# Encoder block with expert-choice experts: first token tiles split and normalized by VectorE alone, base tiles of the final normalization moved from GpSimd's to SyncE's DMA queue

## Chip, cores and metric

One core of a Trainium2 chip runs the whole program in one launch. The metric is the device time of that core in microseconds (us), the median of the runs shown. Five compute engines appear below: TensorE (PE; PEld is its weight load), VectorE (DVE), ScalarE (ACT), GpSimd (POOL) and SyncE (SP), which here issues DMAs only. Each engine works through its own instructions in program order and waits on semaphores of the others.

## What is computed

The input is 2048 tokens of 1024 channels in float32, with 16 learned meta tokens put in front. Cut to what matters here:

```
h    = layer_norm(concat([meta, x]), ln_in_g, ln_in_b)
proj = h @ w_in                       # q, k, v, u, two gates
...                                   # rms-normed q/k, rotary, attention; S5 scan; gated merge
h    = layer_norm(alpha * h + merged @ w_o, ln1_g, ln1_b)
# experts: each of 16 experts takes its 256 best tokens
gate, idx = top_k(softmax(h @ w_router, over tokens), 256)
xe  = h[idx]
ye  = (silu(xe @ w_gate[e]) * (xe @ w_up[e])) @ w_down[e] * gate
moe = zeros.at[idx].add(ye)
out = layer_norm(alpha * h + moe, ln2_g, ln2_b)
```

The changed code is at the two ends: the first layer norm with the first projection, and the last layer norm, which runs beside the last seven experts.

## The kernel before

**Arithmetic.** Float32 matmuls are made of rounded parts: an operand is cast to a high part on ACT (`wh`, `hth`, `xh`, `hh`) and DVE or POOL subtracts it from the original to get the low part (`wl`, `htl`, `xl`, `hl`). Three matmuls (high by high, low by high, high by low) give one product. The step that does this for a weight tile is called a split.

**Start (`phase_a`).** Tokens are worked in 16 tiles of 128 (and one of 16 meta tokens). `load(t)` fetches tile t, `norm(t)` normalizes it on DVE (`ln_ops`, eleven DVE instructions: two statistics, one aggregate, six small ones for the reciprocal root with one ACT square root among them, and two over the whole 128x1024 tile, L106 and L107). `trans(t)` transposes it on PE (L176) and splits the result (L183 ACT, L184 DVE). The projection weight comes in eight row blocks of 768 columns (half 0) and eight of 512 (half 1). `split_w(m, k, eng)` splits block k of half m: cast on ACT (L156), subtraction on `eng` (L157). Tiles 0 and 1 are normalized together, the first three blocks of half 0 are split on POOL and the other five on DVE; then `qkv` runs k by k. Half 1 is split by DVE and POOL in turn while PE works on the first two tiles. A loop over steps s then makes `trans(s+1)`, `norm(s+2)`, `rope(s-1)`, `qkv(s)` and `u_mm` for one tile after another; tile 3 is normalized in step s=1 of this loop.

**Experts.** For each expert e the 12 weight tiles (jobs) of 1 MB each are fetched by SP (`load_w`, L1684), cast on ACT (L1691) and subtracted on DVE (L1692). `ahead(j)` issues load j+3 and split j+2 when PE starts on job j. There are three buffers of the raw tile `wr`, so load j+3 waits on SP until the subtraction of job j is done. Eight steps with gate and up matmuls (L1784) are followed by eight with down matmuls (L1812), two of them for one weight tile. Tokens are gathered (`xg`, L1754) and results added into `acc_d` in DRAM (`scatter`, L1834) by indirect DMAs that POOL issues.

**Side work.** From expert 9 on, `step(e, s)` moves a list of generators on by one piece per PE step. `finish` normalizes the base tiles: all 16 tiles of `acc_d` are loaded (`fx`, L1900), normalized in pairs on ACT (L1874, L1880) and DVE (L1885, L1887) and stored to the output (L1915); a new pair starts every 11 steps, and the next pair's loads are issued in the middle of the pair before. `redo(e)` gathers again the rows that expert e added to (`fa`, L1846), normalizes them and writes them over the output rows (`put_rows`, L1890). For the last expert the same is done by tile in `down_out` (L1818 to L1827).

**What sets the order.** There is no planner: each engine's order is the order in which the code emits instructions, and a DMA is issued by the engine named in front of `dma_start`, in that engine's order. The lines of the change are these:

```
for k in range(3):
    split_w(0, k, PL)
...
if 2 < s + 2 <= NT:
    norm(s + 2)
...
PL.dma_start(xs[t], acc_d[128 * t:128 * t + 128])
...
PL.dma_start(outs[t + i], xs.pop(t + i))
```

Of the kernel before, what the change touches and what calls it, by code (L numbers as in the profile page):

```python
# [28 lines left out]
NT = S // 128  # L29
# [15 lines left out]
def f(t):  # L45
    return t.bitcast(F32)
# [3 lines left out]
def kernel(ctx, tc, x, meta, ln_in_g, ln_in_b, w_in, q_norm_g, k_norm_g,  # L50
# [5 lines left out]
    V, A, PE, PL, SP = nc.vector, nc.scalar, nc.tensor, nc.gpsimd, nc.sync  # L56
    ctx.enter_context(tc.manual_schedule())

    def pool(reuse_waits="tile", **kw):
        return tc.tile_pool(reuse_waits=reuse_waits, **kw)  # L60
# [13 lines left out]
    xs = x[0].rearrange("(c j) d -> j c d", j=T)  # L74
    outs = out[0].rearrange("(c j) d -> j c d", j=T)
# [22 lines left out]
    def ln_ops(pool, t, n, gb, bb, tag):  # L98
        st = pool.tile([128, 2, 6], F32, name=tag + "st", tag=tag + "st")
        mv = pool.tile([128, 2], F32, name=tag + "mv", tag=tag + "mv")  # L100
        r = pool.tile([128, 1], F32, name=tag + "r", tag=tag + "r")
        for i in range(2):
            yield V.bn_stats(st[:n, i], t[:n, 512 * i:512 * i + 512])
        yield V.bn_aggr(mv[:n], st[:n])
        yield from rsqrt_ops(pool, r, mv[:n, 1:2], eps_ln, LN_EPS, 1.0, n, tag)
        yield V.scalar_tensor_tensor(t[:n], t[:n], mv[:n, 0:1], gb[:n], op0=OP.subtract, op1=OP.mult)  # L106
        yield V.scalar_tensor_tensor(t[:n], t[:n], r[:n], bb[:n], op0=OP.mult, op1=OP.add)  # L107
# [5 lines left out]
    def layer_norm(*args):  # L113
        for _ in ln_ops(*args):
            pass

    def phase_a(start_gates):
        cr = ExitStack()
        with ExitStack() as c:
# [4 lines left out]
            sm = c.enter_context(pool(name="a_sm", bufs=3))  # L124
# [3 lines left out]
            X, HT, PQ, QN, RC = {}, {}, {}, {}, {}  # L128
# [10 lines left out]
            gb = wq.tile([128, D], F32, name="gb")  # L139
            bb = wq.tile([128, D], F32, name="bb")  # L140
# [13 lines left out]
            def split_w(m, k, eng):  # L154
                wr = WR.pop(0)
                A.copy(WH[m][:, k], wr)  # L156
                eng.tensor_tensor(WL[m][:, k], wr, f(WH[m][:, k]), op=OP.subtract)  # L157

            def norm(t):
                n = 128 if t < NT else NM  # L160
                layer_norm(sm, X[t], n, gb, bb, "a")
# [8 lines left out]
            def trans(t):  # L170
                n = 128 if t < NT else NM
                if 1 < t < NT:
                    SP.dma_start(h_d[128 * t:128 * t + 128], X[t])
                p = px.tile([128, 8, 128], F32, name="pT")
                for k in range(8):
                    PE.transpose(p[:, k, :n], X[t][:n, 128 * k:128 * k + 128], idf[:n, :n])  # L176
                if t == NT or t % 2 == 0:
                    HT[t // 2] = (hp.tile([128, 8, 256], F32R, name="hth", bufs=3),
                                  hp.tile([128, 8, 256], F32R, name="htl", bufs=3))
                hi, lo = HT[t // 2]  # L180
                o = 128 * (t % 2)
                for k0 in (0, 4):
                    A.copy(hi[:, k0:k0 + 4, o:o + n], p[:, k0:k0 + 4, :n])  # L183
                    V.tensor_tensor(lo[:, k0:k0 + 4, o:o + n], p[:, k0:k0 + 4, :n],  # L184
                                    f(hi[:, k0:k0 + 4, o:o + n]), op=OP.subtract)
                if 1 < t < NT and t % 2 == 1:
                    store_ht(t // 2)
# [5 lines left out]
            def qkv(t, k0, k1):  # L193
                n = 128 if t < NT else NM
                o = 128 * (t % 2)
                hi, lo = HT[t // 2]
                if k0 == 0:
                    PQ[t] = pq.tile([128, 1024], F32, name="pq")
                p = PQ[t]
                for k in range(k0, k1):  # L200
                    for c0, c1 in ((0, 512), (512, 768))[t == NT:]:
                        for i, (a, w) in enumerate(((hi, WH[0]), (lo, WH[0]), (hi, WL[0]))):
                            PE.matmul(p[:n, c0:c1], a[:, k, o:o + n], w[:, k, c0:c1],
                                      start=(k == 0 and i == 0), stop=(k == 7 and i == 2))
# [87 lines left out]
            with pool(name="a_st", bufs=8) as st:  # L292
                for k in range(8):
                    load_w(st, 0, k)
                load(2)
                for _ in zip(*(ln_ops(sm, X[t], 128, gb, bb, "a") for t in range(2))):
                    pass
                for k in range(3):
                    split_w(0, k, PL)
                trans(0)  # L300
                trans(1)
                qkv(0, 0, 2)
                qkv(1, 0, 2)
                for k in range(2, 8):
                    if k > 2:
                        split_w(0, k, V)
                    qkv(0, k, k + 1)
                    qkv(1, k, k + 1)
# [12 lines left out]
                load_w(wr, 1, k)  # L321
            load(3)
            norm(2)
            for k in range(8):
                split_w(1, k, (V, PL)[k % 2])
                if k + 3 < 8:
                    load_w(wr, 1, k + 3)
                if k == 4:
                    load_rope(2)
                    load_rope(3)  # L330
# [4 lines left out]
            for s in range(NT + 4):  # L335
                if s + 4 <= NT:
                    load(s + 4)
                    if s + 4 < NT:
                        load_rope(s + 4)
                if s < NT:  # L340
                    rope_prep(s)
                if 1 <= s < NT:
                    trans(s + 1)
                if 0 <= s - 3 < NT:
                    qk_trans(s - 3, 0)
                next(gg, None)
                if 1 < s <= NT:
                    qkv(s, 0, 3)
                next(gg, None)
                if 0 <= s - 3 <= NT:  # L350
                    qk_trans(s - 3, 1)
                next(gg, None)
                if 2 < s + 2 <= NT:
                    norm(s + 2)
                if 0 <= s - 1 <= NT:
                    rope(s - 1)
                if 1 < s <= NT:
                    qkv(s, 3, 8)
                if 1 <= s <= NT:
                    u_mm((s - 1) // 2, (s - 1) % 2)  # L360
                if s == NT:
                    cr.close()
                    gg = start_gates()
                    next(gg)
                    u_meta()
# [879 lines left out]
    acc_d = dram("acc_d", (S, D), F32)  # L1245
# [291 lines left out]
    E = 16  # L1537
# [133 lines left out]
    def experts(c, pos, inf):  # L1671
# [4 lines left out]
        W, X, XT, HT, IDX, IO, AC = {}, {}, {}, {}, {}, {}, {}  # L1676
# [10 lines left out]
        def split_w(j):  # L1687
            wr = W[j]
            wh = wp.tile([128, 8, 256], F32R, name="wh", bufs=4)
            wl = wp.tile([128, 8, 256], F32R, name="wl", bufs=4)  # L1690
            A.copy(wh, wr)  # L1691
            V.tensor_tensor(wl, wr, f(wh), op=OP.subtract)  # L1692
            W[j] = wh, wl
# [19 lines left out]
        sm = c.enter_context(pool(name="e_m", bufs=2))  # L1713
# [124 lines left out]
        gb = fp.tile([128, D], F32, name="gb2")  # L1838
        bb = fp.tile([128, D], F32, name="bb2")
# [53 lines left out]
        def finish():  # L1893
            SP.dma_start(gb, row_bcast(ln2_g, D))
            SP.dma_start(bb, row_bcast(ln2_b, D))
            xs = {}

            def load(t):
                xs[t] = fp.tile([128, D], F32, name="fx", bufs=4)
                PL.dma_start(xs[t], acc_d[128 * t:128 * t + 128])  # L1900

            yield
            for t in range(2):
                load(t)
            yield
            yield

            def base(t):
                for n, _ in enumerate(norm([xs[t], xs[t + 1]])):
                    if n == 7 and t + 2 < NT:  # L1910
                        load(t + 2)
                        load(t + 3)
                    yield
                for i in range(2):
                    PL.dma_start(outs[t + i], xs.pop(t + i))  # L1915

            yield from pipe((base(t) for t in range(0, NT, 2)), every=MO[3])

# [10 lines left out]
        sides = []  # L1929

        def step(e, s):
            if (e, s) == (E0, 0):
                sides.append(finish())
            if E0 < e < E - 1 and s == MO[0]:
                sides.append(redo(e - 1, MO[1]))
            if (e, s) == (E - 1, 1):
                acc_rows(e)
                sides.append(redo(e - 1, MO[2]))
            for g in sides:
                next(g, None)  # L1940

        one_hot(0, 0, NT)
        pi = pick(0)
# [187 lines left out]
```

## Time and profile before

| what | value |
|---|---|
| median of 3 runs | 3164.89 us (3157.53 to 3165.57) |
| profiled execution, its own time | 3158.51 us |
| its span in the trace | 3156.7 us |
| PE busy | 2978.7 us (94%) |
| DVE busy | 2145.9 us (68%) |
| ACT busy | 1572.0 us (50%) |
| POOL busy | 1010.9 us (32%) |
| DMA bytes | 513.00 MB, mean 163 GB/s |

The profiled execution is 6.4 us shorter than the median. Its own time is 1.8 us more than its span. DMA issue counts as no engine's busy time, so SP has no row. A wait is shown at the instruction behind it, as time its engine sat idle and what ended that.

### The profile page before, as it was taken

Reading aid. Unit: us, or ns where it says so; the run is one execution under the profiler, and the core shown is the slowest. Engines: PE = TensorE matmul, PEld = TensorE weight load, DVE = VectorE, ACT = ScalarE, POOL = GpSimd, SP = SyncE. Lnnn points to the kernel's source line nnn. Section 1 sums busy time; section 2 is a strip of 40 time slices with the busy share of each in tenths; the row PEclk is TensorE's granted clock in tenths of the full one; section 3 lists DMA queues with packets and bytes.
Section 4 is the critical chain, followed back from the end, with each engine's and each line's share of the span. In section 5 each row is a group of like instructions: output and inputs, shape, how many; then the busy total and the mean of one; then the engine's idle time right before and its main releaser. Section 6 shows DMA issues by size and latency. Waiting matters only on the chain.

```text
span 3156.7 us, 56179 instructions
## 1 busy us (share of the span) xinstructions
PE 2978.7 (94%) x22829; PEld 2632.0 (83%) x22829; DVE 2145.9 (68%) x3725; ACT 1572.0 (50%) x2229; POOL 1010.9 (32%) x633
## 2 busy tenths in 40 slices
PE   6999999999989999999899996799999999999997
PEld 5887787777867777777678885699999999999997
DVE  7886589783366666666466666666666665778886
ACT  2222352243369999999622222344444444666553
POOL 3221035051069999999510001111111101122221
PEclk9999999999999999999999998799999999999999
DMA  6566633557510101013366743366677667778884
GB/s 224 186 206 186 160 104 108 185 148 203 175 45 22 35 21 35 21 35 90 110 206 199 200 134 108 134 214 206 214 220 225 217 214 230 258 260 267 274 263 157
DMA packets 464499, 513.00 MB, mean 163 GB/s; under 512 B 47568, under 2 KB 387728, under 8 KB 463856
## 3 DMA queue, kind: packets, MB, share of 16 engines
q1 hardware_dynamic: 433616, 421.20, 42.7%
q0 software_dynamic: 19232, 69.53, 7.3%
q10 hardware_dynamic: 11392, 18.68, 1.7%
q8 instruction: 179, 2.93, 0.4%
q14 instruction: 80, 0.66, 0.1%
HBM read 385.59 MB, written 123.76 MB: 161 GB/s over the span
## 4 chain that ended last, share of the span: by engine, by line
PE 62%; DVE 14%; ACT 8%; DMA 6%; issue 6%; POOL 3%; SPq 1%; ACTq 0%; POOLq 0%; DVEq 0%
PE pg L1784 18%; PE pd L1812 8%; PE pg L1230 7%; PE pw L1383 5%; PE pb L1315 5%; PE pm L449 3%; PE pS L483 3%; ACT pe L490 2%; PE pS L484 2%; PE po L520 2%; DVE wl L1692 2%; PE pz L1147 1%; ACT wh L1691 1%; POOL pl L506 1%; ACT ph L502 1%
## 5 line engine op out<-in xcount | busy, mean ns | idle before, releaser
L1784 PE MATMUL pg<-xh,wh 128*128 128x256 f32 x2048 | 573.0, 280 | 5.5 <-DVE sg L1792 4.6
L1784 PE MATMUL pg<-xh,wl 128*128 128x256 f32 x2048 | 570.3, 278 | 2.8 <-DVE wl L1692 2.8
L1692 DVE TENSOR_TENSOR wl<-wr,wh 128x2048 fp32r<-128x2048 f32 x189 | 433.2, 2292 | 204.2 <-ACT wh L1691 204.1
L1784 PE MATMUL pg<-xl,wh 128*128 128x256 f32 x2048 | 570.6, 279 | 0.0
L506 POOL TENSOR_TENSOR pl<-pe,ph 128x1024 f16<-128x1024 f32 x256 | 542.5, 2148 | 60.5 <-DVE ph L500 48.8
L455 DVE TENSOR_REDUCE mx<-pm 128x1 f32<-128x412 f32 (+1 forms) x640 | 368.6, 586 | 190.1 <-PE pm L449 174.1
L1784 PEld LDWEIGHTS pg<-xh,wh 128*128 128x128 f32 x2048 | 386.6, 189 | 6.3 <-DVE sg L1792 4.8
L1784 PEld LDWEIGHTS pg<-xh,wl 128*128 128x128 f32 x2048 | 385.8, 188 | 3.5 <-DVE wl L1692 3.4
L1784 PEld LDWEIGHTS pg<-xl,wh 128*128 128x128 f32 x2048 | 386.3, 189 | 0.0
L1691 ACT CAST wh<-wr 128x2048 fp32r<-128x2048 f32 x189 | 359.8, 1904 | 16.3 <-DMA wr<-in_w_up_e_dram 9.2
L1230 PE MATMUL pg<-gh,gwh 128*128 128x512 f32 x1024 | 337.0, 405 | 19.5 <-ACT gg L1201 14.1
L490 ACT ACTIVATE pe<-pS,ebias 128x1024 f32<-128x1024 f32 x256 | 284.8, 1112 | 37.9 <-PE pS L484 37.9
L1812 PE MATMUL pd<-wh,hh 128*128 128x256 f32 x1024 | 285.8, 279 | 7.0 <-ACT ye L1831 4.6
L1812 PE MATMUL pd<-wh,hl 128*128 128x256 f32 x1024 | 283.7, 277 | 1.5 <-DVE hl L1799 1.4
L1812 PE MATMUL pd<-wl,hh 128*128 128x256 f32 x1024 | 283.1, 276 | 0.0
L1230 PEld LDWEIGHTS pg<-gh,gwh 128*128 128x128 f32 x1024 | 195.4, 194 | 62.7 <-ACT gg L1201 16.8
L502 ACT CAST ph<-pe 128x1024 f16<-128x1024 f32 x224 | 234.4, 1046 | 16.1 <-ACT pe L490 0.4
L449 PE MATMUL pm<-k,q 128*128 128x412 f32 (+1 forms) x640 | 233.5, 375 | 9.1 <-DVE mx L455 3.1
L483 PE MATMUL pS<-q,k 128*128 128x512 f32 (+1 forms) x544 | 231.8, 426 | 10.6 <-ACT pe L490 9.2
L520 PEld LDWEIGHTS <-ph 128*128 128x128 f16 (+1 forms) x2176 | 188.7, 96 | 63.6 <-issue 60.3
L520 PE MATMUL po<-v,ph 128*128 128x129 f16 (+1 forms) x2176 | 231.5, 221 | 0.8 <-ACT t L528 0.8
L522 PE MATMUL po<-v,pl 128*128 128x65 f16 (+1 forms) x2176 | 220.2, 192 | 2.2 <-POOL pl L506 2.1
(424 smaller groups left out, 6761.5 us busy)
## 6 DMA issues: line engine op xcount, KB each, us to landing
wr<-in_w_gate_e_dram SPq DMA_DIRECT2D x64, 1024.0 KB
wr<-in_w_up_e_dram SPq DMA_DIRECT2D x64, 1024.0 KB
wr<-in_w_down_e_dram SPq DMA_DIRECT2D x64, 1024.0 KB
gwr<-in_w_in_dram SPq DMA_DIRECT2D x32, 512.0 KB
gh<-ht_d SPq DMA_DIRECT2D x64, 256.0 KB
gt_d<-gg ACTq DMA_DIRECT2D x64, 256.0 KB
gt<-gt_d SPq DMA_DIRECT2D x32, 512.0 KB
q<-q_d SPq DMA_DIRECT2D x96, 128.0 KB
```

Source lines behind the costliest of these rows:

```text
L449: PE.matmul(p[:, :w], Q[n][0][:, 128 * j:128 * j + 128], K1[units[n][1] // 4][:, k0:k0 + w], start=True, stop=True)
L455: V.tensor_reduce(MX[n][:, j, c:c + 1], p[:, :w], axis=AX.X, op=OP.max)
L483: PE.matmul(p[:m, a], K2[g][:, k0:k0 + m], Q[n][1], start=True, stop=False)
L490: A.activation(e[:m, :w], p[:m, :w], AF.Exp, bias=ebias[:m], scale=HD ** -0.5)
L502: A.copy(hi[:m, :w], e[:m, :w])
L506: (PL if w == 2 else V).tensor_tensor(lo[:m, :w], e[:m, :w], hi[:m, :w], op=OP.subtract)
L520: PE.matmul(o[:, 0:129], hi[:m, a, 128 * j:128 * j + 128], v16[:m, kt, g, 0:129], start=(kt == 0 and j % 2 == 0), stop=False, skip_group_c ...
L1230: PE.matmul(p, w[:, k], h, start=(k == 0 and j == 0), stop=(k == 7 and j == 2))
L1691: A.copy(wh, wr)
L1692: V.tensor_tensor(wl, wr, f(wh), op=OP.subtract)
L1784: PE.matmul(p[:, gu], w[:, k, cs_], x[:, k], start=(k == 0 and j == 0), stop=(k == 7 and j == 2))
L1812: PE.matmul(p, a[:, k, cs_], w[:, k], start=(k == 0 and j == 0), stop=(k == 7 and j == 2))
```

## The change

Four edits, in two places of the program:

- the first three blocks of weight half 0 are split on DVE instead of POOL, one ahead of `trans(0)`, one between the two transposes and one behind them;
- tile 3's normalization is taken out of the loop and its eleven DVE instructions are emitted two by two behind the splits k = 2 to 7 of weight half 1;
- the loads and stores of the base tiles (16 and 16, 0.5 MB each) are issued by SP instead of POOL, and the first pair's normalization begins four pieces behind its loads instead of two;
- from step 10 of the last expert on, the side work is moved on by two pieces per PE step.

```diff
-                for k in range(3):
-                    split_w(0, k, PL)
+                split_w(0, 0, V)
                 trans(0)
+                split_w(0, 1, V)
                 trans(1)
+                split_w(0, 2, V)
...
+            ln3 = ln_ops(sm, X[3], 128, gb, bb, "a")
             for k in range(8):
                 split_w(1, k, (V, PL)[k % 2])
+                if k > 1:
+                    next(ln3, None)
+                    next(ln3, None)
...
-                if 2 < s + 2 <= NT:
+                if 3 < s + 2 <= NT:
                     norm(s + 2)
...
-                PL.dma_start(xs[t], acc_d[128 * t:128 * t + 128])
+                SP.dma_start(xs[t], acc_d[128 * t:128 * t + 128])
...
-            yield
-            yield
+            for _ in range(4):
+                yield
...
-                    PL.dma_start(outs[t + i], xs.pop(t + i))
+                    SP.dma_start(outs[t + i], xs.pop(t + i))
...
-            for g in sides:
-                next(g, None)
+            for _ in range(2 if (e, s) >= (E - 1, 10) else 1):
+                for g in sides:
+                    next(g, None)
```

The order of instructions at three places follows, first of the kernel before and then of the changed one. Lines of `experts` count five more in the changed kernel (L1684 is L1689, L1692 is L1697, L1887 is L1892, L1900 is L1905, L1915 is L1920).

VectorE before, at the end of the splits of weight half 1 (L157); x_328 is token tile 3, L184 belongs to tile 2's transposes and L217 begins `rope(0)`:

```order
L157 TENSOR_TENSOR wl_97<-wr_353,wh_96 128x512
L157 TENSOR_TENSOR wl_97<-wr_361,wh_96 128x512
L184 TENSOR_TENSOR htl_416<-pT_406,hth_415 128x4x128 x2
L103 BN_STATS ast_421<-x_328 128x6 x2
L104 BN_AGGR amv_422<-ast_421 128x2
L91 TENSOR_SCALAR av_428<-amv_422 128x1
L92 RECIPROCAL ar_423<-as_427 128x1
L93 TENSOR_TENSOR as_427<-ar_423 128x1
L94 TENSOR_TENSOR as_427<-as_427,av_428 128x1
L95 TENSOR_SCALAR as_427<-as_427 128x1
L96 TENSOR_TENSOR ar_423<-ar_423,as_427 128x1
L106 SCALAR_TENSOR_TENSOR x_328<-x_328,amv_422,gb_92 128x1024
```

VectorE in the changed kernel, same place:

```order
L103 BN_STATS ast_357<-x_328 128x6 x2
L104 BN_AGGR amv_358<-ast_357 128x2
L91 TENSOR_SCALAR av_368<-amv_358 128x1
L157 TENSOR_TENSOR wl_97<-wr_353,wh_96 128x512
L92 RECIPROCAL ar_359<-as_367 128x1
L93 TENSOR_TENSOR as_367<-ar_359 128x1
L94 TENSOR_TENSOR as_367<-as_367,av_368 128x1
L95 TENSOR_SCALAR as_367<-as_367 128x1
L157 TENSOR_TENSOR wl_97<-wr_371,wh_96 128x512
L96 TENSOR_TENSOR ar_359<-ar_359,as_367 128x1
L106 SCALAR_TENSOR_TENSOR x_328<-x_328,amv_358,gb_92 128x1024
L107 SCALAR_TENSOR_TENSOR x_328<-x_328,ar_359,bb_93 128x1024
```

Tile 3's normalization moved from behind the low parts of tile 2 (L184) to ahead of them, between the last splits.

SyncE before, at the start of `finish` in expert 9 (the two rows of L1894 and L1895 load the norm's weights, all others are expert weights):

```order
L1684 DMA wr_29697<-in_w_up_e_dram 128x8x256
L1894 DMA gb2_22040<-in_ln2_g_dram 128x1024
L1895 DMA bb2_22041<-in_ln2_b_dram 128x1024
L1684 DMA wr_29809<-in_w_gate_e_dram 128x8x256
L1684 DMA wr_29874<-in_w_up_e_dram 128x8x256
L1684 DMA wr_29935<-in_w_gate_e_dram 128x8x256
```

SyncE in the changed kernel, the same place:

```order
L1899 DMA gb2_22040<-in_ln2_g_dram 128x1024
L1900 DMA bb2_22041<-in_ln2_b_dram 128x1024
L1689 DMA wr_29809<-in_w_gate_e_dram 128x8x256
L1905 DMA fx_29866<-acc_d 128x1024
L1905 DMA fx_29868<-acc_d 128x1024
L1689 DMA wr_29874<-in_w_up_e_dram 128x8x256
```

SyncE in the changed kernel, at the second pair's loads and the first pair's stores:

```order
L1689 DMA wr_30362<-in_w_gate_e_dram 128x8x256
L1689 DMA wr_30435<-in_w_up_e_dram 128x8x256
L1905 DMA fx_30471<-acc_d 128x1024
L1905 DMA fx_30473<-acc_d 128x1024
L1689 DMA wr_30507<-in_w_gate_e_dram 128x8x256
L1920 DMA out_0_dram<-fx_29866 128x1024
L1920 DMA out_0_dram<-fx_29868 128x1024
L1689 DMA wr_30577<-in_w_up_e_dram 128x8x256
```

Loads and stores of base tiles now stand between the loads of expert weights, two and two, eight times each.

VectorE in the changed kernel, around the last instruction of the first pair, for which the second of those stores waits (wr_30362, wr_30435 and wr_30507 are three expert weight tiles in a row, and the load of wr_30577 takes the buffer of wr_30362):

```order
L1697 TENSOR_TENSOR wl_30438<-wr_30362,wh_30437 128x2048
L1728 TENSOR_SCALAR oh_30441<-slot_22035,pos_21631 128x256
L1728 TENSOR_SCALAR oh_30443<-slot_22035,pos_21631 128x256
L1892 SCALAR_TENSOR_TENSOR fx_29866<-fx_29866,fr_30116,bb2_22041 128x1024
L1728 TENSOR_SCALAR oh_30476<-slot_22035,pos_21631 128x256
L1728 TENSOR_SCALAR oh_30478<-slot_22035,pos_21631 128x256
L1890 SCALAR_TENSOR_TENSOR fx_29868<-fx_29868,fm_30114,gb2_22040 128x1024
L1697 TENSOR_TENSOR wl_30510<-wr_30435,wh_30509 128x2048
L1728 TENSOR_SCALAR oh_30513<-slot_22035,pos_21631 128x256
L1728 TENSOR_SCALAR oh_30515<-slot_22035,pos_21631 128x256
L1892 SCALAR_TENSOR_TENSOR fx_29868<-fx_29868,fr_30116,bb2_22041 128x1024
```

The pair's last instruction stands behind the subtraction of wr_30435, one split later than the one that the load of wr_30577 itself needs; in the kernel before it stood there too, and the store that needs it was POOL's.

## Rows read from the trace of the kernel before

**Rows 1.** The page: share of the span in the chain that ended last.

```profile
PE 62%; DVE 14%; ACT 8%; DMA 6%; issue 6%; POOL 3%; SPq 1%; ACTq 0%; POOLq 0%; DVEq 0%
```

**Rows 2.** Stretches: us, busy PE PEld DVE ACT POOL, clock, DMA share, GB/s.

```profile
2440.00:2600.00 160.00, 160.00 (x1450) 159.93 (x1450) 101.39 (x141) 75.80 (x92) 15.77 (x8) 1.00 0.70 218
2660.00:2670.00 10.00, 7.00 (x39) 7.00 (x40) 6.83 (x9) 7.28 (x12) 0.00 (x0) 0.66 0.44 161
2800.00:2860.00 60.00, 55.29 (x498) 54.05 (x497) 45.72 (x83) 38.14 (x53) 13.69 (x11) 1.00 0.84 286
3000.00:3060.00 60.00, 57.85 (x517) 56.63 (x518) 48.12 (x80) 35.33 (x48) 13.36 (x11) 1.00 0.84 272
```

**Rows 3.** PE at the start: start, us, line, operation, [idle before, what ended it].

```profile
55.09 1.94 PE L176 MATMUL pT<-idf,x 128*128 128x128 f32 x8 [4.30 <-DVE x L107]
58.75 0.77 PE L203 MATMUL pq<-wh,hth 128*128 128x512 f32 x1 [1.73 <-DVE sq L232]
```

**Rows 4.** DVE at the start, same columns.

```profile
12.15 5.57 DVE L107 SCALAR_TENSOR_TENSOR x<-x,ar,bb 128x1024 f32<-128x1024 f32 x2
...
43.99 0.69 DVE L157 TENSOR_TENSOR wl<-wr,wh 128x512 fp32r<-128x512 f32 x1 [2.96 <-ACT wh L156]
...
47.12 1.28 DVE L103 BATCH_NORM_STATS2 ast<-x 128x6 f32<-128x512 f32 x2
...
50.59 1.46 DVE L94 TENSOR_TENSOR as<-as,av 128x1 f32<-128x1 f32 x1
...
53.65 1.28 DVE L107 SCALAR_TENSOR_TENSOR x<-x,ar,bb 128x1024 f32<-128x1024 f32 x1
```

**Rows 5.** Waits of POOL from 2600 us on: total us, times, longest.

```profile
POOL out_dram L1915 <- DVE fx L1887: 112.0, 9, 42.1
...
POOL fx L1900 <- DMA acc_d<-ye,ix: 24.8, 3, 9.0
```

**Rows 6.** First base pair: the chain that ended last (start, us, what).

```profile
2642.71 9.59 DMA acc_d<-ye,ix
```

**Rows 7.** First base pair on ACT, and the weight cast ahead of it.

```profile
2647.87 1.90 ACT L1691 CAST wh<-wr 128x2048 fp32r<-128x2048 f32 x1
...
2659.00 1.06 ACT L1874 ACTIVATE fj<-fx 128x1024 f32<-128x1024 f32 x1 [8.93 <-DMA fx<-acc_d]
```

**Rows 8.** Waits of PE from 2440 us on: total us, times, longest.

```profile
PE pg L1784 <- DVE sg L1792: 4.6, 1, 4.6
```

**Rows 9.** Weight loads as SP issues them: start, us, line.

```profile
2634.93 0.38 SPq L1684 DMA_DIRECT2D wr<-in_w_up_e_dram  x1
...
2695.10 0.37 SPq L1684 DMA_DIRECT2D wr<-in_w_gate_e_dram  x1
...
2797.23 0.37 SPq L1684 DMA_DIRECT2D wr<-in_w_up_e_dram  x1
```

**Rows 10.** DVE at the end of the first base pair.

```profile
2692.78 2.29 DVE L1692 TENSOR_TENSOR wl<-wr,wh 128x2048 fp32r<-128x2048 f32 x1
...
2700.75 1.29 DVE L1887 SCALAR_TENSOR_TENSOR fx<-fx,fr,bb 128x1024 f32<-128x1024 f32 x1
```

**Rows 11.** ACT, two casts that waited for their weights.

```profile
2809.65 1.91 ACT L1691 CAST wh<-wr 128x2048 fp32r<-128x2048 f32 x1 [2.85 <-DMA wr<-in_w_up_e_dram]
...
2816.53 1.91 ACT L1691 CAST wh<-wr 128x2048 fp32r<-128x2048 f32 x1 [4.28 <-DMA wr<-in_w_down_e_dram]
```

**Rows 12.** DMA from 2600 us on: SP's queue, POOL's queue, base loads' median landing.

```profile
q1 hardware_dynamic: 88688, 90.18, 49.6%
q0 software_dynamic: 12384, 45.09, 24.7%
...
fx<-acc_d POOLq DMA_DIRECT2D x16, 512.0 KB, 7.7
```

**Rows 13.** The end: POOL's last row store, with its wait.

```profile
3149.54 0.95 POOL L1890 DMA_INDIRECT out_dram<-ye,io  x1 [3.12 <-DMA out_dram<-ye,io]
```

**Rows 14.** The end: DVE's last instruction.

```profile
3144.31 1.28 DVE L1827 SCALAR_TENSOR_TENSOR ye<-ye,lr,bb 128x1024 f32<-128x1024 f32 x1
```

## Prediction

> **What bounds the kernel now.** I read the page first. The chain that ended last is 62% PE, with DVE at 14% and ACT at 8% [rows 1]: TensorE is the limit, and time is won or lost only where it waits or runs at a lower clock. So I went to the two stretches that the change touches and looked for PE's waits there, not at the engines' shares.
>
> At the start PE waits twice behind VectorE: 4.30 us for tile 3's last normalizing instruction, and 1.73 us for the rotary step that stands behind it on DVE [rows 3]. That normalization runs on DVE from 47.12 to 54.93 us, 7.8 us in all, and it is stretched: a small instruction takes 1.46 us beside POOL's work, and the two big ones of tiles 0 and 1 take 5.57 us, 2.79 each, against 1.28 alone [rows 4].
>
> In the experts PE is full up to 2600 us: 160.00 busy of 160.00 [rows 2]. Behind that come the base tiles, and PE loses 4.7 of 60 us in one stretch and 2.2 of 60 in another, at full clock [rows 2]. The longest single wait is 4.6 us, when ACT stood 8.93 us before the first base tile [rows 7, 8]; the 10 us around its end were granted 0.66 of the clock, so some 4 us of matmuls ran at 1.2 instead of 2.4 GHz, about 2 us lost. The pair of 8.93 and 4.6 also says how much delay of ACT the matmuls hide: 4.3 us.
>
> **Start, edits 1 and 2.** Moving three splits to DVE frees tiles 0 and 1 from POOL: the 5.57 us should become two of 1.28 [rows 4], 3 us sooner, less a split of 128x768, about 1.0 us by the 0.69 us of a 128x512 one [rows 4], that stands ahead of the first transposes. So PE begins some 2 us earlier. I count this as nothing: the later splits already wait for weights (DVE idle 2.96 us before the one at 43.99, until ACT's cast [rows 4]), so PE arrives sooner at weights that are not sooner there. Bounds 0 and 2 us of gain.
>
> Of tile 3's 7.8 us, the first eight instructions now fall into DVE's idle time between the splits. The last three (a small one and two of 1.28 us, 2.7 us) still stand between the last split and the low parts of tile 2, as the order shows. That leaves 7.8 - 2.7 = **5.1 us gain**. If both big ones run beside POOL at 2.79 us they take 5.6, and 2.2 us remain; the most is PE's two waits, 6.0 us. The work from there on is a full pipeline of PE and DVE, so I expect the gain to be kept.
>
> **First base pair, edit 3.** SP now stands at the first base load until the scatter lands at 2642.71 + 9.59 = 2652.3 us [rows 6]. Queued behind it is an expert weight that was issued at 2634.93 and cast at 2647.87 [rows 7, 9]. It now goes out near 2653.1, with 1.05 MB of base tiles ahead of it and 1.05 MB of its own. At 286 GB/s [rows 2] that is 7.3 us, so it lands at 2660.4, 12.5 us after its cast was due. PE hides 4.3 and loses 8.2. In return ACT no longer stands before a base tile that is not there (two pieces more of delay), and 4.6 + 2 us come back. Net **+2 us** (from -6.6, if the weight comes in time, to +4, if the clock falls here too).
>
> **The other seven pairs, edit 3.** A store pair on SP waits for the pair's last DVE instruction, which stands one split later than what the next weight load needs. In the trace that instruction ended at 2700.75 + 1.29 = 2702.04, while the weight behind it was issued at 2695.10, right after its split (2692.78 + 2.29) [rows 9, 10]. So the weight goes out 6.9 us late, and the second store, 0.52 MB at 286 GB/s, puts 1.8 us ahead of it: 8.7 us. All later weights stand behind it on SP, and ACT, in order, holds the activations behind a cast that waits.
>
> What can cover this? In a quiet stretch the weight is cast 12.9 us after its issue [rows 7, 9]; 1.05 MB at 218 to 286 GB/s [rows 2] takes 3.7 to 4.8 us, so some 8 us are spare, and with PE's 4.3 nearly all is hidden. I take 1 us for such a pair (0 to 4.4). In a burst of scatters, gathers and base tiles nothing is spare: a weight issued at 2797.23 had its cast only at 2809.65, after a wait of 2.85, and the next waited 4.28 [rows 9, 11]. There 8.7 - 4.3 = 4.4 us are lost (0 to 8.7). How many pairs meet a burst? From 2600 to 3157 us there is one per expert, 557 / 6.5 = 86 us apart, over 20 us long by [rows 11], and a pair has two places on SP, its loads and its stores; the loads can also stand behind a scatter, as POOL did three times for 24.8 us together [rows 5]. Two chances of a quarter to a third make about a half: four of seven. 4 x 4.4 + 3 x 1 = **+21 us** (0 to 45).
>
> **What POOL gives back, edit 3.** POOL stood 112 us in nine waits before base stores [rows 5], with scatters and gathers queued behind them. They will go out sooner and less bunched, and 16 loads and 16 stores leave its queue. The two bursts that I looked at cost PE 4.7 and 2.2 us [rows 2], partly for other reasons. I take **-4 us** (0 to -9).
>
> A base load took 7.7 us to land from POOL's queue [rows 12]; no row shows one issued by SP. The Trainium skill ("DMA: Bandwidth & Descriptors", section "Issuing engine by pattern") gives simple loads and stores to SyncE and calls its path generally faster; from its first-byte figures ("Latency and other measured facts", 0.6 and 1 us) I estimate 0.4 us per pair of loads, 3 us in all, which would make the sum +9 instead of +12. The trace weighs more on the other side: what is at stake is not how fast SP moves a tile but what stands behind it.
>
> In SP's queue a packet is 90.18 MB / 88688 = 1.0 KB, in POOL's 3.6 KB [rows 12]. The same page ("Queues, rings and completion order") says that each DMA engine takes turns between its queues packet by packet. By that rule POOL's queue gets 3.6 bytes for one of a weight's while both have work, and taking the base tiles out of it would end much of the bursts; the time would then be that of the first rival below.
>
> **The end, edit 4.** The last row store on POOL went out at 3149.54 after 3.12 us for the one before it, while DVE was done at 3144.31 + 1.28 = 3145.59 [rows 13, 14]. With the last redo ahead of the last two tiles, its stores leave earlier and this wait can go: at most 3.9 us. But DVE's work is only reordered, so I take **-2 us** (0 to -3.9).
>
> **Sum.** -5 + 2 + 21 - 4 - 2 = +12. The profiled execution took 3158.5 us, so 3170.5 by it. It lies 6.4 us under the median of the runs, 3164.9; against that the forecast is **3177 us**.
>
> **Rivals.**
>
> Faster: the spare 8 us hold everywhere, because without the base tiles in POOL's queue there are no bursts in which weights come late. For it: in a quiet stretch no cast waits, and SP would be 8.7 us late against 8 spare and 4.3 hidden. Against it: scatters and gathers stay in POOL's queue, and the first pair's SP wait of 18 us is longer than any cover. Then -5 - 6.6 - 4.7 - 2.2 - 2 = -20.5, so 3144 us by the median.
>
> No difference that shows: only two pairs meet a burst (2 x 4.4 + 5 x 1 = 14, which gives +5), or only one and the first pair comes free; a weaker start (2.2 instead of 5.1, edit 2 not doing what it says because POOL's splits stretch the two big instructions) pulls it up again. 3163 to 3172 us.
>
> Much slower: the burst of each of the seven pairs is met, and after each PE wait the clock falls as it did at the first pair, 2 us more. 7 x (4.4 + 2) = 45 in place of 21, so +36: 3201 us. It decides from the point at which PE idles over 4 us at a time. For it: it did so at the only wait of that length [rows 2, 8]. Against it: PE's other losses, in the later stretches, came at full clock [rows 2].
>
> **How the numbers follow.** A measurement of this kernel tells 0.3% from no change, 9.5 us. Chances: forecast 0.54, faster rival 0.17, no difference 0.15, much slower 0.14. Of the forecast's 0.54 some 0.06 lies within 9.5 us. So faster 0.17, same 0.21, slower 0.62. The range takes in the forecast with its bounds, the weaker half of the faster rival and most of the slow one: 3148 to 3203 us.
>
> **What would show it.** Right: PE's wait for tile 3 at the start is gone and `rope(0)` ends about 5 us sooner. The wait of 8.93 us before the first base tile is gone, and in its place ACT's cast waits near 2653 for a weight. SP waits for base tiles' last DVE instructions and for scatters, and behind them casts wait for weights several times, with PE idle for 3 to 9 us each. Wrong: casts that wait for no weight behind SP's stores; then slack covers them, and the faster rival holds. Wrong too if the weights issued late land in time because the bursts are gone, or if the start keeps its two waits.

## The result, and the profile after

The changed kernel takes 3194.62 us (median of 4 runs, 3191.32 to 3198.33) against 3163.55 us (4 runs): a ratio of 1.0102, 95% interval 1.0082 to 1.0121, or 32 us more (26 to 38). It was forecast to become slower by 12 us, so the direction was right and the size was not: the loss is between two and three times the forecast. The time lies inside the range that was given.

The profiled execution took 3191.32 us, its span is 3189.5 us. The page's shares of the chain that ended last, where [rows 1] had 62% for PE and 6% for DMA, and the first lines of its list of groups (line, engine, tiles, times; busy us, mean ns; idle before and what ended most of it):

```profile
PE 58%; DVE 14%; DMA 9%; ACT 8%; issue 7%; POOL 3%; SPq 1%; ACTq 0%; POOLq 0%; DVEq 0%
...
L1789 PE MATMUL pg<-xh,wh 128*128 128x256 f32 x2048 | 577.6, 282 | 35.5 <-ACT wh L1696 19.3
...
L1696 ACT CAST wh<-wr 128x2048 fp32r<-128x2048 f32 x189 | 359.8, 1904 | 102.1 <-DMA wr<-in_w_up_e_dram 57.0
```

The last of these shows where the loss begins: ScalarE's cast of expert weights now waits 102.1 us for weights; before it was 16.3 us. PE waits 35.5 us ahead of its first gate and up matmuls, before 5.5 us.

The stretches, with the columns of [rows 2]:

```profile
2600.00:2660.00 60.00, 52.41 (x473) 51.88 (x472) 31.25 (x51) 24.70 (x29) 7.79 (x4) 0.93 0.70 214
2800.00:2860.00 60.00, 49.66 (x411) 48.90 (x409) 36.35 (x73) 33.81 (x46) 1.91 (x2) 0.91 0.68 228
2860.00:3000.00 140.00, 119.12 (x1033) 117.20 (x1034) 99.32 (x168) 68.50 (x92) 29.35 (x16) 0.94 0.79 257
3000.00:3060.00 60.00, 51.66 (x434) 50.65 (x434) 42.38 (x86) 30.23 (x43) 12.80 (x6) 0.93 0.62 200
```

In each stretch PE is idle for 8 to 21 us, and in each the granted clock is 0.91 to 0.94, where [rows 2] had 1.00 in the two that it shows: behind the long waits of PE some matmuls ran at 1.2 GHz (behind the longest they took 0.41 us each, later 0.28). The same 22829 matmuls were 2978.7 us busy before and are 2988.7 us busy now, so some 10 us of the loss are clock, by one execution of each; the rest is waiting.

The four waits of PE over 4 us (start, us, what; in brackets idle before):

```profile
2655.64 0.58 PE L1789 MATMUL pg<-xh,wh 128*128 128x256 f32 x1 [6.06 <-ACT wh L1696]
2818.60 0.55 PE L1789 MATMUL pg<-xh,wh 128*128 128x256 f32 x1 [9.13 <-DVE sg L1797]
2885.03 0.58 PE L1789 MATMUL pg<-xh,wh 128*128 128x256 f32 x1 [11.10 <-ACT wh L1696]
3055.89 0.55 PE L1789 MATMUL pg<-xh,wh 128*128 128x256 f32 x1 [4.88 <-DVE sg L1797]
```

Each stands behind a cast on ACT that had waited for its weight, 11.79, 13.27, 18.88 and 10.18 us.

What SP waited for from 2600 us on (total us, times, longest), its base loads (L1905) and base stores (L1920):

```profile
SPq L1905 <- DMA acc_d<-ye,ix: 49.2, 6, 13.7
SPq L1920 <- DMA out_dram<-fa,io: 43.3, 2, 25.2
...
SPq L1920 <- DVE fx L1892: 32.0, 4, 10.0
SPq L1920 <- DVE sg L1796: 29.7, 3, 11.1
```

Six waits for scatters into `acc_d` and some 86 us for DVE (these two rows and six smaller ones) were expected. The second row was not: base stores waited for row stores `out<-fa`, by which POOL writes the redone rows of an earlier expert into the same output tensor.

One such place, step by step. SP (start, us, line), then POOL's row store, DVE's last instructions on the row tile (`fa`) and on the pair (`fx`), the cast on ACT that stood behind SP's stores, and the chain that ended last:

```profile
2846.33 0.38 SPq L1689 DMA_DIRECT2D wr<-in_w_gate_e_dram  x1
2872.02 1.14 SPq L1920 DMA_DIRECT2D out_dram<-fx  x2
2873.25 1.64 SPq L1689 DMA_DIRECT2D wr<-in_w_up_e_dram  x1
```

```profile
2864.03 5.56 POOL L1895 DMA_INDIRECT out_dram<-fa,io  x1 [61.64 <-DVE oh L1728]
```

```profile
2862.47 1.28 DVE L1892 SCALAR_TENSOR_TENSOR fa<-fa,fr,bb 128x1024 f32<-128x1024 f32 x1
...
2864.06 1.28 DVE L1892 SCALAR_TENSOR_TENSOR fx<-fx,fr,bb 128x1024 f32<-128x1024 f32 x1
```

```profile
2883.08 1.90 ACT L1696 CAST wh<-wr 128x2048 fp32r<-128x2048 f32 x1 [18.88 <-DMA wr<-in_w_up_e_dram]
```

```profile
2864.03 7.92 DMA out_dram<-fa,io
...
2873.25 9.76 DMA wr<-in_w_up_e_dram
```

The row store went out 0.28 us after DVE had finished its rows (2862.47 + 1.28 = 2863.75), so it had waited for those, although the page names the instruction behind. The pair was done on DVE at 2865.34 us, but SP's store went out at 2872.02, when the row store had landed (2864.03 + 7.92). The expert weight behind it, which would otherwise have gone out at 2853.34 after its split, went out at 2873.25: 20 us late, not 8.7. ACT stood 18.88 us at its cast, and PE was idle for the 11.10 us shown above.

The start, with the columns of [rows 3]:

```profile
56.29 0.47 PE L203 MATMUL pq<-wh,hth 128*128 128x512 f32 x1 [3.45 <-DVE sq L232]
```

The wait of 4.30 us for tile 3 is gone; the one behind it grew from 1.73 to 3.45 us. PE comes to this matmul 2.46 us sooner than in [rows 3].

At the first base pair, ACT no longer waits for a base tile ([rows 7] had 8.93 us), but for the weight behind the two loads:

```profile
2653.69 1.90 ACT L1696 CAST wh<-wr 128x2048 fp32r<-128x2048 f32 x1 [11.79 <-DMA wr<-in_w_up_e_dram]
```

### The profile page after: what moved, and what is told of

The parts are those of the page before. It is cut to its first block, busy times and chain, and to the rows that moved or that the text cites. A ratio compares the mean times of both kernels' runs of the same rounds, so it can differ in the third digit from the quotient of the medians.

```text
span 3189.5 us, 56193 instructions
## 1 busy us (share of the span) xinstructions
PE 2988.7 (94%) x22829; PEld 2642.2 (83%) x22829; DVE 2147.5 (67%) x3728; ACT 1572.5 (49%) x2229; POOL 986.1 (31%) x598
## 4 chain that ended last, share of the span: by engine, by line
PE 58%; DVE 14%; DMA 9%; ACT 8%; issue 7%; POOL 3%; SPq 1%; ACTq 0%; POOLq 0%; DVEq 0%
PE pg L1789 15%; PE pd L1817 7%; PE pg L1235 7%; PE pw L1388 5%; PE pb L1320 5%; PE pm L454 3%; PE pS L488 3%; ACT pe L495 2%; PE pS L489 2%; PE po L525 2%; DVE wl L1697 2%; ACT wh L1696 1%; DMA acc_d<-ye,ix 1%; PE pz L1152 1%; POOL pl L511 1%
## 5 line engine op out<-in xcount | busy, mean ns | idle before, releaser
L1697 DVE TENSOR_TENSOR wl<-wr,wh 128x2048 fp32r<-128x2048 f32 x189 | 433.1, 2292 | 266.7 <-ACT wh L1696 266.2
L1789 PE MATMUL pg<-xh,wh 128*128 128x256 f32 x2048 | 577.6, 282 | 35.5 <-ACT wh L1696 19.3
L1696 ACT CAST wh<-wr 128x2048 fp32r<-128x2048 f32 x189 | 359.8, 1904 | 102.1 <-DMA wr<-in_w_up_e_dram 57.0
L1839 POOL DMA_INDIRECT acc_d<-ye,ix x30 | 65.1, 2169 | 528.5 <-ACT ye L1836 517.3
```

The costliest lines, as they stand in the source:

```text
L1789: PE.matmul(p[:, gu], w[:, k, cs_], x[:, k], start=(k == 0 and j == 0), stop=(k == 7 and j == 2))
```

## Experiments

Two theories stood against each other. **Q**: the loss is made on SP, where expert weights stand behind the waits of base tiles. **R**: it comes from the pairs' later start, by which their work on ACT and DVE meets that of the redone rows. In the short diffs `SP` and `PL` are the engines that issue.

**Base tiles back on POOL.** The changed kernel with this alone undone:

```diff
-                SP.dma_start(xs[t], acc_d[128 * t:128 * t + 128])
+                PL.dma_start(xs[t], acc_d[128 * t:128 * t + 128])
...
-                    SP.dma_start(outs[t + i], xs.pop(t + i))
+                    PL.dma_start(outs[t + i], xs.pop(t + i))
```

> The changed kernel with the base tiles' loads and stores back on POOL's queue; the start, the four pieces of delay and the double steps stay. Theory Q (the loss is made on SP, where expert weights stand behind waits of base tiles): the loss of the expert stage goes, the gains stay: -6 at the start, -5 for the wait of 8.9 us before the first base tile, -4 at the end, so about 3149 us (3143 to 3156), ratio 0.995. Rival R (the loss comes from the later start of the pairs, whose DVE and ACT work now meets that of the rows redone): it stays near the changed kernel, 3180 or more.

Measured: 3154.01 us (7 runs), ratio 0.9972 (0.9957 to 0.9986). ACT's casts waited 3.0 us for weights from 2600 us on, in two waits:

```profile
ACT wh L1696 <- DMA wr<-in_w_down_e_dram: 1.8, 1, 1.8
ACT wh L1696 <- DMA wr<-in_w_up_e_dram: 1.2, 1, 1.2
```

R by itself falls: the pairs begin as late here, and the loss is gone. The price of SP's queue is 1.0102 - 0.9972 = 0.0130, 41 us, and the other edits together gain 9 us (4 to 14), where the forecast had 13.6 for them (5 + 6.6 + 2).

**SP's queue alone.** The kernel before, with only those two lines changed.

> The kernel before with only the base tiles' loads and stores moved to SP. Theory Q: the whole loss of the expert stage, +38 (+25 to +50), 3190 to 3215 us. Rival R: no delay is changed, so within 0.3% of before, 3155 to 3173.

Measured: 3192.13 us (4 runs), ratio 1.0091 (1.0076 to 1.0106). Q again, at the low end of its range: the two lines by themselves make a loss of 29 us. But it is not the same loss as in the changed kernel, where they cost 41. What SP waited for here from 2600 us on, before base loads (L1900) and base stores (L1915):

```profile
SPq L1900 <- DMA acc_d<-ye,ix: 64.5, 5, 20.0
SPq L1915 <- DVE sg L1791: 40.9, 5, 12.5
...
SPq L1915 <- DVE fx L1887: 34.9, 6, 7.6
```

With three smaller rows the waits for DVE come to 107 us, and there is no wait for a row store. With two pieces of delay the stores of the fourth and of the seventh pair go out ahead of POOL's row stores (2860.76 and 3028.21 us, row stores at 2873.95 and 3039.97); with four pieces they stand behind them. So the 43.3 us of waits for row stores take both: the later start puts those base stores behind the row stores, and SP's queue makes the expert weights wait for it. That much of R, that the later start makes the pairs meet the redone rows, is true together with Q. In the kernel with the base tiles on POOL the same order cost POOL 10.2 us in two waits. Whether the whole difference of 12 us (about 3 to 21) between 41 and 29 is this was not tried.

**The start alone** (edits 1 and 2 on the kernel before).

> The kernel before with the two edits at the start alone. By the trace of the changed kernel, which reaches the first expert split 6.1 us sooner: -6 us, about 3157.5 us (3155 to 3161). If that lead is lost again before the end: 3163.

Measured: 3163.41 us (12 runs), ratio 1.0001 (0.9991 to 1.0012). The 6 us were read from one execution, which begins its first expert subtraction at 2013.17 us, against 2019.24 in the kernel before. The four profiled executions of kernels without the two edits begin it at 2016.6 to 2021.9 us, the ten with them at 2011.8 to 2017.9: single executions differ there by 5 to 6 us in code that is the same. On average the ten are 4.9 us ahead (about 2 to 8). Earlier the lead is plain: in the first 250 us the four start 1451 to 1456 matmuls, the ten 1471 to 1484, some 3 to 4 us of work at the rate there. In the run time a lead of 3 us (0.001) is at the edge of the interval; the expected 6 us and the forecast's 5 lie outside. So the lead is there at 250 us, and that it lasts to the end is not shown.

**The double steps alone** (edit 4 on the kernel before).

> The kernel before with the double steps of the last redo alone. Expected from the last row store's wait of 3.12 us and the one before it: -2 (-4 to 0), 3159 to 3163.5 us. By the trace of the changed kernel, which gains 6 us between its last weight split and the end, up to -6, 3157.

Measured: 3161.63 us (12 runs), ratio 0.9995 (0.9983 to 1.0007). No difference that this can tell; -2 is inside.

**The four pieces of delay alone** on the kernel before:

```diff
-            yield
-            yield
+            for _ in range(4):
+                yield
```

> The kernel before with only the first pair's normalization begun four pieces behind its loads instead of two. If the wait of 8.9 us of ACT before the first base tile, with the clock that falls behind it, is the gain of the kernel with the base tiles on POOL: -7 us, about 3157 (3153 to 3160), and PE near 2700 us of the kernel before some 7 us early. If the delay only moves the wait: 3163.

Measured: 3161.02 us (12 runs), ratio 0.9987 (0.9976 to 0.9999), 4 us less. In its trace the wait of 8.93 us before the first base tile is gone. So the delay gains; 6.6 us, what PE had lost there, is inside the interval (0.3 to 7.6 us), and so is next to nothing.

Then the price of SP's queue was taken apart.

**Only the loads, or only the stores, on SP** (the changed kernel with the other of the two lines back on `PL`).

> The changed kernel with the base tiles' stores back on POOL and their loads left on SP. In the changed kernel SP waited 49.2 us in six waits for scatters before base loads, and PE's idle times behind those (near 2656, 2819 and 2983) come to some 20 us. Theory L (loads behind scatters make about half of the loss): about 3154 + 18 = 3172 us (3166 to 3180). Rival S (the stores make nearly all of it): 3158 or less. Rival, neither alone: 3185 or more.

Measured: 3186.18 us (4 runs), ratio 1.0064 (1.0042 to 1.0086). That is above the range of theory L. The time lies in the range of the rival "neither alone", by the ratio (3183.8 us) just short of it.

> The changed kernel with the base tiles' loads back on POOL and their stores left on SP. In the changed kernel SP waited 43.3 us in two waits for row stores of the redone rows and some 85 us for DVE before base stores; PE's idle times behind them (near 2886, 2983 and 3056) come to some 20 us. Theory L and S in equal parts: about 3172 us (3166 to 3180). Rival S: 3185 or more.

Measured: 3178.43 us (9 runs), ratio 1.0041 (1.0025 to 1.0057), in the range of L and S together. Against the kernel with all base tiles on POOL (0.9972) the loads cost 0.0092, 29 us, and the stores 0.0069, 22 us. Neither is nearly all of it. Together they are 51 us, more than the 41; a weight that is late for one need not be late again for the other, but the intervals of these runs leave room for no difference at all. By ratios both lie above the halves of 18 us that were expected, the loads clearly; the medians of these runs and of the two that follow are some 5 us higher, and so are those of the kernel before that was timed beside them (3168.48 us).

**Redone rows into a tensor of their own.** The changed kernel; the final rows that `redo` and the last expert write are missing from its output:

```diff
-            PL.indirect_dma_start(out=out[0], out_offset=...
+            PL.indirect_dma_start(out=o2_d, out_offset=...
```

> The changed kernel, but the rows that are normalized again go to a DRAM tensor of their own and not into the output (so the output misses them): no base store waits for a row store. If the two waits of 25.2 and 18.1 us for row stores are behind the idle times near 2886 and 3056 us: about 15 us less, 3180 us (3174 to 3185). If DVE's last instruction of the pair alone sets when the stores go: no change, 3190 to 3199.

Measured: 3183.74 us (4 runs), ratio 1.0057 (1.0035 to 1.0079): 0.0045 or 14 us less than the changed kernel. SP's waits of 43.3 us for row stores are gone from its trace, while its waits for DVE before base stores rise from 86 to 118 us: where both were waited for, DVE's is left. That is the size expected. The edit also frees POOL's row stores from base stores (16.2 us in two waits of the changed kernel), which is not priced apart.

**Base tiles loaded from a tensor that nothing adds to.** The changed kernel; the base tiles of its output lack what the experts add:

```diff
-                SP.dma_start(xs[t], acc_d[128 * t:128 * t + 128])
+                SP.dma_start(xs[t], h1_d[128 * t:128 * t + 128])
```

> The changed kernel, but base tiles are loaded from the normalized stream h1_d, which nothing adds to, instead of from acc_d (so the output lacks what the experts add): no base load waits for a scatter. If the six waits for scatters make half of the loss: about 18 us less, 3177 us (3170 to 3183). If only what stands in the queue in bytes matters: no change, 3190 to 3199.

Measured: 3175.18 us (10 runs), ratio 1.0030 (1.0018 to 1.0042): 0.0072 or 23 us less, in the range expected. By these figures the waits for scatters are the largest part.

**Both of these together**: on SP only the waits for DVE are left, and the bytes.

> The changed kernel with base tiles loaded from h1_d and the redone rows stored to a tensor of their own (the output lacks both): SP's base tiles wait for DVE only. This prices the term of the forecast alone (stores behind the pair's last DVE instruction, +21 us for the seven pairs) against the kernel with the base tiles on POOL, ratio 0.9972. By the forecast's term: 0.9972 + 0.0066 = 1.004, some 3178 us. If the two runs that took away one wait each add up (0.0045 and 0.0072 less than 1.0102): 0.9985, some 3160 us, and the term was less than 5 us.

Measured: 3163.40 us (10 runs), ratio 0.9993 (0.9981 to 1.0005). The two parts add up nearly (0.0109 of 0.0045 + 0.0072). What stays above the kernel with the base tiles on POOL is 0.9993 - 0.9972 = 0.0021, 7 us (about 1 to 13), and that is the term which the forecast put at 21; 1.004, what its term would give, is outside the interval. What the two edits free on POOL is not priced apart here either. SP still waited 119 us for DVE before base stores in this run (the first row below and six smaller ones), and ACT's casts too, in 21 waits of at most 6.6 us:

```profile
SPq L1921 <- DVE fx L1893: 66.1, 8, 10.9
...
ACT wh L1697 <- DMA wr<-in_w_up_e_dram: 24.3, 9, 5.2
ACT wh L1697 <- DMA wr<-in_w_gate_e_dram: 23.6, 8, 6.6
ACT wh L1697 <- DMA wr<-in_w_down_e_dram: 15.1, 4, 6.5
...
PE pg L1790 <- ACT wh L1697: 4.3, 2, 2.4
```

63 us of casts that waited became 4.3 us of PE waiting for a cast. All waits of PE from 2600 us on come to 27.5 us here and to 20.4 in the kernel with the base tiles on POOL, 7 us apart like the times. So waits of up to 6.6 us nearly vanish behind the matmuls, while in the changed kernel one of 18.88 us cost 11.1.

**Stores two pieces later.** The changed kernel:

```diff
+                for _ in range(2):
+                    yield
                 for i in range(2):
                     SP.dma_start(outs[t + i], xs.pop(t + i))
```

> The changed kernel with each pair of base stores emitted two pieces later on SP, so that the pair's last DVE instruction is done when SP comes to them. If SP's wait for that instruction, which was the main term of the forecast, makes a good part of the loss: 10 us less or more, 3185 us or under. If scatters and row stores make it: 3 us less or nothing, 3189 to 3198.

Measured: 3189.63 us (4 runs), ratio 1.0083 (1.0064 to 1.0102). SP's waits for DVE before stores fell from some 86 to 37 us and those for row stores from 43.3 to 23.3 us, and the time fell by 6 us. As a difference that is between the two expectations, the time itself lies in the second, and the intervals of the two kernels overlap. It fits the small price of the waits for DVE but shows little by itself.

**POOL's rotary tables earlier.** The kernel with the base tiles on POOL, in which `rope(0)` on DVE runs beside POOL's L166 and L167 for tiles 0 and 1:

```diff
                 split_w(1, k, (V, PL)[k % 2])
+                if k == 1:
+                    rope_prep(0)
+                    rope_prep(1)
...
-                if s < NT:
+                if 1 < s < NT:
                     rope_prep(s)
```

> The kernel with the base tiles on POOL, and POOL's preparation of the rotary tables of tiles 0 and 1 (L166, L167) emitted behind the split k = 1 of weight half 1 instead of in the loop, so that rope(0)'s DVE chain does not run beside it. If that work of POOL eats half of the start's gain: PE at 100 us of the kernel before some 5 to 6 us early instead of 3, and 3 us less in all, about 3151. If not: 3 us early as before, 3154.

Measured: 3153.18 us (6 runs), ratio 0.9964 (0.9951 to 0.9976), not to be told from 0.9972. PE's first rotary matmul came at 57.05 us, later than the 55.66 of the kernel it is made from, though its wait shrank from 2.98 to 0.85:

```profile
57.05 0.47 PE L203 MATMUL pq<-wh,hth 128*128 128x512 f32 x1 [0.85 <-DVE sq L232]
```

```profile
PE pu L267 <- POOL wl L157: 4.0, 3, 2.4
```

The expectation failed. DVE's chain to L232 did run free again (53.14 to 56.90, 3.8 us as before), but the tables pushed POOL's splits back, and PE waited 4.0 us for those.

## Why the forecast was wrong in size

By its own steps:

**What bounds the kernel, and the cover.** Right. PE is the limit, and what counts is how late a weight comes. "PE hides 4.3" was the low end: of the casts' waits of 11.79, 13.27, 18.88 and 10.18 us, PE idled for 6.06, 9.13, 11.10 and 4.88, so 4.1 to 7.8 us were hidden, and waits up to 6.6 us cost almost nothing.

**Start, -5.** Direction right, mis-sized: PE is 2.5 us early at its first rotary matmul (3.1 with the base tiles on POOL), with the wait behind tile 3 grown from 1.73 to 3.45 us. The step that failed is the one that let the whole wait go. `rope(0)` on DVE began at 50.04 instead of 54.85 us, 4.8 us sooner, as worked out; but there POOL still made its rotary tables (46.89 to 53.97 us), and the chain to L232 took 6.1 us instead of 3.8. Two of its small instructions waited for POOL (they end at 52.52 and 54.00 us, two of POOL's at 52.48 and 53.97), as the 1.46 us row in [rows 4] does:

```profile
50.90 1.62 DVE L91 TENSOR_SCALAR qv<-ss 128x10 f32<-128x10 f32 x1
...
52.66 1.34 DVE L93 TENSOR_TENSOR qs<-rs 128x10 f32<-128x10 f32 x1
```

I had asked what the moved normalization would run beside, not what the work that moves up behind it would. Which of edits 1 and 2 the lead belongs to was not tried apart.

**First base pair, +2.** Right in what happens. The cast waited 11.79 us for its weight (12.5 forecast), PE was idle for 6.06 and 1.53 us (8.2 forecast), and the 8.93 us before the first tile are gone. The clock fell here too, to 0.93 up to 2660 us and 0.89 in the 10 us behind, which the forecast kept for its upper bound of +4. What the gone wait gives back is 4 us by the delay alone (0.3 to 7.6), where 6.6 were taken.

**The other seven pairs, +21.** This is the term that failed, in three ways. First, the waits that it priced are cheap: stores behind the pair's last DVE instruction cost 7 us in all, since waits of some 7 us are hidden even when several follow each other. The rule "in a burst nothing is spare" was wrong as a price. Second, it put the order between base stores and row stores at nothing. Both write the output, and a base store that comes behind a row store waits until that has landed. In the kernel before no wait of a base store names a row store; the two pieces of delay, which the forecast counted as a gain only, moved two pairs' stores behind row stores. With the base tiles on POOL that costs nobody but POOL; on SP the expert weights wait with them: 14 us. Third, scatters were priced at the first pair only; for the others they were a chance to meet a burst, at the price of a wait for DVE. Six waits came, and they cost 23 us with the first pair among them.

**Clock.** The forecast kept the fall of the clock for its slow rival ("it decides from the point at which PE idles over 4 us at a time"). PE idled over 4 us at four places (6.1, 9.1, 11.1 and 4.9 us), the clock fell in all four stretches, and 10 us more of PE's busy time are the price (2987 to 2989 us in the three profiled executions with all base tiles on SP and their waits left in, 2975 to 2983 in the six with all on POOL). That part of the rival came true.

**What POOL gives back, -4.** Not seen apart. With the loads and stores on SP, POOL's idle times before row stores are longer (222.4 us in four waits, where 51.6 us were), but they say little: base tiles no longer stand between them, and each of the four ended 0.28 us after DVE had finished the rows to be stored. Only two further waits, 16.2 us, name base stores on SP.

**The end, -2.** Right in mechanism. With the base tiles on POOL the last row store goes out 0.3 us after DVE's last instruction, where [rows 13, 14] have 3.95 us:

```profile
3143.63 0.95 POOL L1895 DMA_INDIRECT out_dram<-ye,io  x1 [4.87 <-DVE ye L1832]
```

```profile
3142.07 1.28 DVE L1832 SCALAR_TENSOR_TENSOR ye<-ye,lr,bb 128x1024 f32<-128x1024 f32 x1
```

The runs of this edit alone (0.9983 to 1.0007) hold -2 and hold nothing as well.

**The sum.** Forecast: 25 us of price on SP (8.2 + 21 - 4) against 13.6 of gains by the other edits (5 + 6.6 + 2). Measured: 41 against 9. Both errors go the same way. The time lies inside the range only because that took in most of the much slower rival (a burst at each of the seven pairs, and the clock). Of this the clock came true; the waits were others, so that it held is luck.

**SP's path and the turns of the queues.** The Trainium skill ("DMA: Bandwidth & Descriptors", section "Issuing engine by pattern") gives simple loads and stores to SyncE; here that does not pay: with the two lines alone the time rises by 0.0091. How fast SP's tiles land no run shows by itself; the runs show that what stands behind the tiles is worth more. By the turn-taking by packets that the same page of the Trainium skill states ("Queues, rings and completion order") the bursts would have ended and the faster rival held; no run with base tiles on SP came faster than with them on POOL.

**A version that is faster than both.** The changed kernel with its base tiles back on POOL: 0.9972 (0.9957 to 0.9986).

## What to carry to other kernels

Before a DMA moves to another engine's queue, list every wait that the DMA itself carries (here for compute, for scatters into the tensor that it reads, and for other stores into the tensor that it writes): on the new queue each of them stands in front of whatever that queue feeds. Do it for the order of the changed program: a second edit, here two pieces of delay, can add a wait that the old order did not have. Price a late load not by its lateness but by what is left beyond the cover: 119 us of waits for DVE, none over 11, cost 7 us, while 92 us of waits for other DMAs, in 8 pieces of up to 25 us, cost 34. When work moves up in time, look at what the other engines do in the new place, also for the work that moves up behind it.

## What was not expected of the hardware

A DVE instruction with one small tensor input (L91, 128x10) took 1.62 us beside POOL's table work of 1.56 to 1.57 us each, against 0.17 us in the kernel before: it was held for about one whole POOL instruction, as instructions with two inputs were. Three of the ten profiled executions with edits 1 and 2 show it (1.60 to 1.62 us); in the others L91 took 0.17 us. In all nine in which the tables lie beside `rope(0)` two small instructions are held, in six of them L93 and L94 (1.02 to 1.03 and 1.45 to 1.47 us) in place of L91 and L93. What decides which was not tried.
